# Attention scores as two products of 128 rows: the keys' low part stored twice

## The chip, the core and the metric

The kernel runs on one core of a Trainium2 chip. The core has a matrix engine (TensorE, PE in the profile; its weight loads are a queue of their own, PEld), a vector engine (DVE), a scalar engine (ACT), GpSimd (POOL) and a sync engine (SP) that issues transfers. The metric is the device time of one execution in microseconds (us); for the kernel before, the median of three runs is 3030.7 us (3026.78 to 3032.99).

## What is computed

Two blocks follow each other on 512 latent tokens of width 1024. Block 1 has two layers. Each layer modulates the normed latents and 256 context tokens, projects them, and mixes them by a global attention, a windowed attention with a sink and a short convolution; a mixture of 16 experts follows, in which each expert chooses its tokens. The context has its own mixer and experts in layer 0 alone. Block 2 has a banded attention with a sink, a dilated attention, gates and an output product. The attention at the heart of block 1 is:

```python
def attend(q, k, v, mask, sink):
    s = jnp.einsum('bqkgd,bskd->bkgqs', q, k, preferred_element_type=jnp.float32) * (HEAD_DIM ** -0.5)
    if mask is not None:
        s = jnp.where(mask, s, NEG_INF)
    ...
        p = jax.nn.softmax(s, axis=-1)
    return jnp.einsum('bkgqs,bskd->bqkgd', p.astype(v.dtype), v)
```

Heads have 64 columns (HEAD_DIM = 64). Everything is float32.

## The kernel before

A float32 factor is split into a high and a low part, both in PE's faster float32r format, and a product is made of three: high by high, low by high, high by low (`mm3`, L204 to L206). The scores do this with fewer products. A head has only 64 rows, so one tile of 128 rows holds two parts of the query, stacked: its high part in one half of the partitions and its low part in the other (`q_block`, L465 and L466). The keys' high part is stored twice, in both halves (`k_parts`, L475 and L476), so that one product of 128 rows gives high by high plus low by high (L520). The keys' low part is stored once, in the half in which the query's high part lies (L477), and a second product of 64 rows adds high by low (L521). `row` names that half.

A unit of attention is one head and one tile of 128 queries. `scores` makes its row of scores in PSUM (tile S, two buffers), segment by segment: the latents have two segments a unit (latent keys of 256 to 512 columns, context keys of 256), the context and block 2 have one. A vector operation finds the maximum (L531, or L527 with the mask), ACT takes the exponential (L535 or L537), and DVE or ACT scales the rows (L542 or L544) into P. `turn` transposes P on PE (L140) and ACT copies the result (PT, L563); `pv` multiplies it with the values (L611). `section` runs the units one after the other, with each unit's transposes one unit later, and spreads fillers between them: projections of the next heads, the convolution, the merge of branches. Their weights come by transfers from SP (L191) and are split on ACT (L183) and DVE (L184).

The program text gives the order in which work is offered. A scheduler in the framework may move instructions on an engine by its own costs; each engine runs its list in order. The context's keys and values are made in the latents' pass (`lat_start`), written to DRAM on POOL's queue (L816) and read back for the context's own pass (L671); `key_parts` lists what is written.

Of the kernel before, what the change touches and what calls it, by code (L numbers as in the profile page):

```python
# [18 lines left out]
D = 1024  # L19
KT = 8  # L20
# [9 lines left out]
class Stream:  # L30
    """One of the two token streams: latents or context."""
# [6 lines left out]
class Kernel:  # L38
# [43 lines left out]

    def dense_psum(self, mm=2, s=1024):
        """Banks for products (mm), for scores of s columns (2 tiles) and for transposes (2)."""
        es = ExitStack()
        tc = self.tc
        self.s_cols = s
        self.p_mm = es.enter_context(tc.tile_pool(name="p_mm", bufs=mm, space=PSUM, reuse_waits="tile"))
        self.p_s = es.enter_context(tc.tile_pool(name="p_s", bufs=2, space=PSUM, reuse_waits="tile"))
        self.p_t = es.enter_context(tc.tile_pool(name="p_t", bufs=2, space=PSUM, reuse_waits="tile"))  # L90
        return es
# [14 lines left out]
    def blend(*parts):  # L106
        """The steps of several (generator, steps), spread evenly over each other."""
# [22 lines left out]
    def copy(self, out, in_):  # L130
        """A plain copy, on the scalar engine and the vector engine in turn."""
# [10 lines left out]
    def rsqrt(self, ss, shape, mul, eps):  # L142
        """(ss * mul + eps) ** -0.5 and the radicand, by Newton's iteration."""
# [21 lines left out]
    def exp(self, pool, out, x, w):  # L165
        """exp(x) for x <= 0 on the vector engine, to float32's accuracy: 2^k * e^r, |r| <= ln(2) / 2."""
# [14 lines left out]
    def split(self, src, hi, lo):  # L181
        """src = hi + lo, both in the 12 significant bits of float32r."""
        self.nc.scalar.activation(hi, src, ACTF.Copy)  # L183
        self.nc.vector.tensor_sub(lo, src, hi.bitcast(FP32))  # L184

    def wblock(self, pool, src):
        """A block of weights [K, 256]: per 512 rows its two float32r parts [128, 4, 256]."""
# [10 lines left out]
    def mm3(self, ps, lhs, rhs, lsel, rsel):  # L198
        """ps = sum over k tiles of lhs^T rhs, each a list of two parts by k tile."""
# [70 lines left out]
    def adaln(self, l, r, pool):  # L270
        """Columns r * 2048 to (r + 1) * 2048 of both streams' modulation of layer l, in 17 steps."""
# [35 lines left out]
    def ada_load(self, l, r, pool, *tiles):  # L307
        """Loads pieces [128, 1024] of w_ada, unless they are there."""
# [7 lines left out]

    def affine_cols(self, name, gname, gi, l, s, kinds):
        """The per-channel scale g * (1 + sc) and shift of a modulated norm."""
# [8 lines left out]
    def norm(self, xt, junk, xn=None):  # L327
        """Token-major rows scaled by their rsqrt of the mean square, in place or into xn; the last tile's on its own."""
# [9 lines left out]
    def scale(self, out, in_, col, i):  # L338
        """Rows by a column, on the vector engine and the scalar engine in turn."""
# [17 lines left out]
    def hT(self, pool, h, xn, G, S):  # L357
        """The modulated norm of a stream, channel-major, in two parts; KT steps."""
# [21 lines left out]
    def hT_raw(self, raw, xn):  # L380
        """The norm without its modulation, channel-major."""
# [14 lines left out]

    def rope_tab(self, pool, name, g, tab):
        """Rope's tables with a norm's gain folded in: [128, 4, 64] for x and for its swapped halves."""
# [12 lines left out]
    def heads_block(self, pool, ps, dst, ss, t, nh, tabs, g):  # L411
        """dst = rope(ps * g) for nh heads of one token tile; ss = their sums of squares."""
# [21 lines left out]
    def q_block(self, out, pool, xp, wp, src, h, st, tabs, g, sink, kv=None):  # L434
        """Four query heads, in five steps: two tiles [128, 2, n] of stacked parts, scales and sinks.

        The high parts lie in half kv, or head by head in one and the other.
        """
# [32 lines left out]
    def k_parts(self, tp, kh, kl, j):  # L471
        """Head j of the transposed keys tp [128, n] into the doubled parts kh, kl [128, n]."""
# [4 lines left out]
        nc.vector.tensor_sub(kl[a], tp[a], kh[a].bitcast(FP32))  # L477

    def k_block(self, pool, kr, ss, nt, nh, kh, kl):
        """Normalises the roped keys kr [128, nt, nh * 64] and writes their parts."""  # L480
# [11 lines left out]
    def kv_block(self, pool, w, h, st, tabs, g, kh, kl, V, kr=None):  # L492
        """Two key heads and two value heads of a stream from a block [ka | va] of w_in."""
# [14 lines left out]

    def scores(self, pool, q, row, t, segs, region, mask, sc, skc, mult):
        """Softmax of one head and query tile: its rows [128, keys].  # L510

        row: the rows of the high parts of the queries and the low parts of the keys; segs: (score
        column, key parts, key column, width); region: the score columns in use.
        """
# [4 lines left out]
        for at, kh, kl, k0, w in segs:  # L519
            nc.tensor.matmul(S[:, at:at + w], lhs, kh[:, k0:k0 + w], start=True, stop=False)  # L520
            nc.tensor.matmul(S[:, at:at + w], lhs[row], kl[row, k0:k0 + w], start=False, stop=True)  # L521
# [25 lines left out]
    def turn(self, P, c0, slots, PT, qc):  # L547
        """P's key tiles, transposed, into PT[:, slot, qc:qc + 128]; slots: (score column, slot)."""
# [17 lines left out]
    def section(self, groups, fillers, last=False):  # L566
        """Runs groups of attention units with other work between them.

        groups: an iterable of (units, finish); a unit: (rows, then), where rows() emits the scores
        and the softmax and then(rows) the transposes, which come one unit later; finish comes one  # L570
        step behind the last unit of its group. fillers: (generator, steps).
        """
# [30 lines left out]
    def pv(self, PTs, plans):  # L603
        """O^T [128 = two heads, 256]; a plan: (slot, values, first column, end) by key tile."""
# [11 lines left out]

    def mixer(self, l, st, src, csrc, dst, ahead=None):
        """x + gt1 * mixer(modulated norm of x) for one stream, then the router's choice.

        ahead: how many slots of expert weights to open at the start, behind the attention, behind  # L620
        the merge and behind the projection.
        """
# [110 lines left out]
    def close_above(es, k):  # L733
        """Closes the pools of a stack above its first k."""
# [7 lines left out]
    def lat_start(self, l, wp, xp, kp, h, K, src, csrc):  # L742
        """The latents' modulated norm and keys and values, and the context's; its parts go to DRAM for its own pass."""
# [4 lines left out]
        with ExitStack() as es:  # L748
# [26 lines left out]
            def keys():  # L775
                """Four blocks of keys and values, each one's end behind the next one's products."""
# [48 lines left out]
    def key_parts(K):  # L825
        """The written parts of two branches' keys and values."""
        return [x for kh, kl, V in K for x in (kh, kl[0:64, 0], kl[64:128, 1], V)]
# [9 lines left out]
    def ring_open(self, side, k, first=False):  # L837
        """Opens k slots; with first, the first one lies behind the others."""
# [8 lines left out]
    def ring_fill(self):  # L847
        """Loads into the slots that are open, one a step."""
# [4 lines left out]
    def ring_load(self):  # L853
        """Loads the next half of an expert's matrix into the next slot."""
# [27 lines left out]
    def attention(self, b, kv, ap, qd, K, KC, mask, o, n):  # L882
        """The groups of one attention branch's four heads that share keys: two pairs of heads into o."""
# [7 lines left out]
        def unit(PTs, pr, j, half, ti):  # L891
# [28 lines left out]
            def rows():  # L920
                return self.scores(ap, q[pr][:, j], slice(64 * kv, 64 * kv + 64), t, segs, r, msk,
# [62 lines left out]
    def merge(self, l, st, wp, p, h, W, b, o, acc, step, xp=None, mg=None):  # L984
        """acc += 2 * sigmoid(gate b) * (o @ w_branch[b]); at the last step the halved sum's parts."""
# [30 lines left out]
    def project(self, l, st, wp, p, mg, src, dst, ring, extra):  # L1016
        """x + gt1 * (merged @ w_out), its norm and the router's softmax over the experts [tokens, NE].

        The softmax has the latents' tiles in the order 0, 2, 1, 3.
        """  # L1020
# [20 lines left out]
        def shift():  # L1041
            """The router's share of the norm's shift and its weights with the scale."""
# [6 lines left out]
        def rows(t):  # L1049
            """A tile's logits and normalised rows, in two steps."""  # L1050
# [60 lines left out]
    def choose(self, l, st, p, z):  # L1111
        """Each expert's tokens and gates (halved), by slots: in columns, or as scatter and gather indices.
# [498 lines left out]
```

## Time and profile before

| | |
|---|---|
| median of the runs | 3030.7 us |
| span of the profiled execution | 3023.8 us |
| PE busy | 2895.2 us (96%) |
| PE weight loads busy | 1866.4 us (62%) |
| DVE busy | 1415.6 us (47%) |
| ACT busy | 957.7 us (32%) |

The profile is of one execution, whose own time is given as its span, from the first instruction to the last. The shares are means over stages that differ: attention stands at 135 to 535 us (latents, layer 0), 720 to 880 (context), 1646 to 2046 (latents, layer 1) and 2780 to 2995 (block 2); the experts, with their large weight transfers, lie between. A PE that is shown as busy need not be at its peak, since products overlap and their ends are modelled; what a product costs in a row of products is the distance from its start to the next one's.

### The profile page before, as it was taken

To read this page: it belongs to the slowest core of one execution; us is meant where nothing else is said; L and a number is where in the kernel's file an instruction comes from. 1 tells how busy PE (TensorE), PEld (TensorE's weight loads), DVE (VectorE), ACT (ScalarE), POOL (GpSimd) and SP (SyncE) were. 2 spreads that over 40 slices of the span, in tenths; PEclk is the share of its full clock that TensorE was granted. 3 is DMA by queue.
4 is the path that set the end of the run, shared out by engine and by line. 5 is a ranking of instruction groups with operands and counts; after the bars stand their busy time and mean duration, and the time that the engine had idled before them with its cause. 6 is when DMAs were issued, how large, how long until landed. Compare 5 with 4: busy or idle time off the path is not lost.

```text
span 3023.8 us, 45171 instructions
## 1 busy us (share of the span) xinstructions
PE 2895.2 (96%) x18117; PEld 1866.4 (62%) x18117; DVE 1415.6 (47%) x3807; ACT 957.7 (32%) x1950; POOL 110.1 (4%) x135
## 2 busy tenths in 40 slices
PE   7999999999998999999979999999799999889999
PEld 3777777678895443433347777778744433338878
DVE  4655565348764111111146555654523232237885
ACT  4444454224552000000044444543200000015663
POOL 0100000011001011100000000000000000000000
PEclk8999999999998999999999999999899999999999
DMA  8321111668457999999573211114689999953221
GB/s 296 123 69 56 56 42 50 206 210 308 136 174 255 389 403 397 402 395 368 180 262 116 68 56 56 43 53 141 260 348 397 414 361 363 370 196 107 57 84 57
DMA packets 272646, 629.24 MB, mean 208 GB/s; under 512 B 24324, under 2 KB 148948, under 8 KB 272436
## 3 DMA queue, kind: packets, MB, share of 16 engines
q1 hardware_dynamic: 259396, 595.31, 53.5%
q0 software_dynamic: 12016, 27.86, 3.2%
q8 instruction: 143, 2.34, 0.3%
q10 hardware_dynamic: 1024, 3.18, 0.3%
q14 instruction: 67, 0.55, 0.1%
HBM read 606.30 MB, written 19.99 MB: 207 GB/s over the span
## 4 chain that ended last, share of the span: by engine, by line
PE 73%; issue 14%; DMA 6%; DVE 4%; ACT 1%; SPq 0%; POOL 0%; POOLq 0%; ACTq 0%; DVEq 0%
PE mm L204 13%; PE mm L205 12%; PE mm L206 12%; PE au L1217 8%; PE tp L140 5%; PE yp L1243 4%; PE S L521 4%; PE mm L611 4%; DMA x<-ylat,silat 4%; PE S L520 3%; PE S L282 3%; PE tx L1330 2%; PE yp L1348 1%; DVE xt L1350 1%; PE S L1038 1%
## 5 line engine op out<-in xcount | busy, mean ns | idle before, releaser
L204 PE MATMUL mm<-hhi,whi 128*128 128x512 f32 (+1 forms) x928 | 341.6, 368 | 0.0
L184 DVE TENSOR_TENSOR wlo<-wraw,whi 128x1024 fp32r<-128x1024 f32 x234 | 285.7, 1222 | 107.0 <-ACT whi L183 102.4
L206 PE MATMUL mm<-hhi,wlo 128*128 128x512 f32 (+1 forms) x928 | 335.1, 361 | 0.0
L205 PE MATMUL mm<-hlo,whi 128*128 128x512 f32 (+1 forms) x928 | 333.6, 360 | 0.0
L183 ACT ACTIVATE whi<-wraw 128x1024 fp32r<-128x1024 f32 x234 | 247.1, 1059 | 185.5 <-PE mm L205 106.7
L1243 PE MATMUL yp<-we,hT 128*32 128x256 f32 (+1 forms) x2016 | 294.2, 496 | 10.3 <-ACT hT L134 4.9
L1217 PE MATMUL au<-we,xT 128*64 128x512 f32 x1024 | 236.5, 597 | 0.0
L204 PE MATMUL mm<-whi,hhi 128*128 128x256 f32 x736 | 218.8, 298 | 10.6 <-ACT qr L423 6.6
L1217 PE MATMUL au<-we,xTlat 128*64 128x512 f32 x960 | 227.1, 599 | 0.3
L205 PE MATMUL mm<-wlo,hhi 128*128 128x256 f32 x736 | 212.8, 290 | 2.1 <-DVE wlo L184 2.1
L206 PE MATMUL mm<-whi,hlo 128*128 128x256 f32 x736 | 212.5, 290 | 0.0
L1243 PEld LDWEIGHTS yp<-we,hT 128*32 128x32 f32 (+1 forms) x2016 | 99.1, 124 | 182.4 <-issue 144.5
L563 ACT ACTIVATE PT<-tp 128x384 f32<-128x384 f32 (+2 forms) x392 | 142.6, 407 | 211.6 <-PE tp L140 209.7
L204 PEld LDWEIGHTS mm<-hhi,whi 128*128 128x128 f32 x928 | 176.3, 190 | 32.1 <-issue 4.4
L206 PEld LDWEIGHTS mm<-hhi,wlo 128*128 128x128 f32 x928 | 176.0, 190 | 25.9 <-issue 1.1
L205 PEld LDWEIGHTS mm<-hlo,whi 128*128 128x128 f32 x928 | 176.3, 190 | 24.9 <-issue 1.5
L535 ACT ACTIVATE P<-S,mx,sc 128x768 f32<-128x768 f32 (+5 forms) x192 | 151.9, 792 | 70.9 <-DVE mx L532 67.6
L204 PEld LDWEIGHTS mm<-whi,hhi 128*128 128x128 f32 x736 | 143.0, 194 | 26.9 <-ACT qr L423 8.5
L1217 PEld LDWEIGHTS au<-we,xT 128*64 128x64 f32 x1024 | 70.6, 137 | 129.2 <-issue 126.1
L205 PEld LDWEIGHTS mm<-wlo,hhi 128*128 128x128 f32 x736 | 143.0, 195 | 5.4 <-DVE wlo L184 2.7
L206 PEld LDWEIGHTS mm<-whi,hlo 128*128 128x128 f32 x736 | 142.7, 194 | 4.0 <-issue 2.8
L1226 ACT ACTIVATE th<-au 128x512 f32<-128x512 f32 (+1 forms) x47 | 24.6, 524 | 378.3 <-PE au L1217 378.3
(326 smaller groups left out, 4830.5 us busy)
## 6 DMA issues: line engine op xcount, KB each, us to landing
we<-in_w_e_gate_dram SPq DMA_DIRECT2D x128, 1024.0 KB, 11.5
we<-in_w_e_up_dram SPq DMA_DIRECT2D x128, 1024.0 KB, 11.1
we<-in_w_e_down_dram SPq DMA_DIRECT2D x128, 1024.0 KB, 11.0
wraw<-in_w_in_dram SPq DMA_DIRECT2D x166, 512.0 KB, 3.7
wada<-in_w_ada_dram SPq DMA_DIRECT2D x96, 512.0 KB, 6.1
wraw<-in_w_branch_dram SPq DMA_DIRECT2D x36, 512.0 KB, 3.4
wraw<-in_w_out_dram SPq DMA_DIRECT2D x32, 512.0 KB, 3.9
xt<-in_x_dram SPq DMA_DIRECT2D x8, 512.0 KB, 9.2
```

Of the source, the lines that this page charges most:

```text
L140: self.nc.tensor.transpose(out, in_, self.ident[:p, :p])
L183: self.nc.scalar.activation(hi, src, ACTF.Copy)
L184: self.nc.vector.tensor_sub(lo, src, hi.bitcast(FP32))
L204: nc.tensor.matmul(ps, lh, rh, start=k == 0, stop=False)
L205: nc.tensor.matmul(ps, lh, rl, start=False, stop=False)
L206: nc.tensor.matmul(ps, ll, rh, start=False, stop=k == n)
L521: nc.tensor.matmul(S[:, at:at + w], lhs[row], kl[row, k0:k0 + w], start=False, stop=True)
L535: nc.scalar.activation(P, S[:, c0:c1], ACTF.Exp, bias=mx[:, 1:2], scale=sc, accum_out=mx[:, 2:3])
L563: self.nc.scalar.activation(PT[:, s0:s0 + j - i, qc:qc + 128], tp[:, i * 128:j * 128].rearrange("p (s c) -> p s c", c=128), ACTF.Copy)
L611: nc.tensor.matmul(O[64 * j:64 * j + 64, a:b], v, PTs[j][:, slot, a:b], start=i == 0, stop=i == last, skip_group_check=True)
L1217: self.nc.tensor.matmul(ps[j * st.cap:(j + 1) * st.cap], st.xT[:, kt, s0:s0 + st.cap], w[kt // 4][:, kt % 4, j * st.w:(j + 1) * st.w], sta ...
L1243: self.nc.tensor.matmul(ps[o * st.cap:(o + 1) * st.cap], hT[:, j * 128 + q * st.cap:j * 128 + (q + 1) * st.cap], w[kt // 4][:, kt % 4, o * ...
```

## The change

`k_parts` writes the keys' low part into both halves, with a second subtraction, and the second score product takes all 128 rows of the query tile and of the low part. It then adds high by low and also low by low. `row` goes away, and the third entry of block 2's key lists with it. `key_parts` now names the whole low tile, so that two transfers of one half each become one of both halves, for the store and for the load.

```diff
@@ k_parts
         nc.scalar.activation(kh[b], tp[a], ACTF.Copy)
         nc.vector.tensor_sub(kl[a], tp[a], kh[a].bitcast(FP32))
+        nc.vector.tensor_sub(kl[b], tp[a], kh[b].bitcast(FP32))
@@ scores
-    def scores(self, pool, q, row, t, segs, region, mask, sc, skc, mult):
+    def scores(self, pool, q, t, segs, region, mask, sc, skc, mult):
...
         for at, kh, kl, k0, w in segs:
             nc.tensor.matmul(S[:, at:at + w], lhs, kh[:, k0:k0 + w], start=True, stop=False)
-            nc.tensor.matmul(S[:, at:at + w], lhs[row], kl[row, k0:k0 + w], start=False, stop=True)
+            nc.tensor.matmul(S[:, at:at + w], lhs, kl[:, k0:k0 + w], start=False, stop=True)
@@ key_parts
-        return [x for kh, kl, V in K for x in (kh, kl[0:64, 0], kl[64:128, 1], V)]
+        return [x for kh, kl, V in K for x in (kh, kl, V)]
@@ attention, rows
-                return self.scores(ap, q[pr][:, j], slice(64 * kv, 64 * kv + 64), t, segs, r, msk,
+                return self.scores(ap, q[pr][:, j], t, segs, r, msk,
@@ block2
-                    segs = [(a0, *K[hh][:2], loc[0] * 128, w_)]
+                    segs = [(a0, *K[hh], loc[0] * 128, w_)]
...
-                out.append(list(zip(kh, kl, (0, 1, 0, 1))))
+                out.append(list(zip(kh, kl)))
```

Below line 477 the changed kernel's line numbers are higher by one, and from the score products on by two: L520 becomes L522, L521 L523, L611 L613.

The numbers of products, loads and transposes on PE are the same, and over most of the program their order too. DVE has 26 instructions more, POOL four transfers fewer. In a few places the scheduler sets things in another order. On DVE, in block 2's first section of attention (kx are the keys of the second four heads, tp their transposes, S and mx a unit's scores and maximum), before:

```order
L484 TENSOR_TENSOR qr<-qr,rsq 128x1024
L538 SCALAR_TENSOR_TENSOR P,mx<-P,mulB 128x128
L540 RECIPROCAL mx<-mx 128x1
L477 TENSOR_TENSOR kx<-tp,kx 64x512
L527 ISA S,mx<-S,maskB 128x128
L527 ISA mx 128x1
L532 TENSOR_SCALAR mx<-mx,sc 128x1
L477 TENSOR_TENSOR kx<-tp,kx 64x512 x3
L417 TENSOR_REDUCE qss<-sq 128x4
```

and now:

```order
L477 TENSOR_TENSOR kx<-tp,kx 64x512
L478 TENSOR_TENSOR kx<-tp,kx 64x512
L477 TENSOR_TENSOR kx<-tp,kx 64x512
L478 TENSOR_TENSOR kx<-tp,kx 64x512
L477 TENSOR_TENSOR kx<-tp,kx 64x512
L478 TENSOR_TENSOR kx<-tp,kx 64x512
L477 TENSOR_TENSOR kx<-tp,kx 64x512
L478 TENSOR_TENSOR kx<-tp,kx 64x512
L417 TENSOR_REDUCE qss<-sq 128x4
L529 ISA S,mx<-S,maskB 128x128
L529 ISA mx 128x1
```

The mask of the unit of 128 columns (L527, now L529) stood behind the first head's subtraction and stands now behind all eight.

On PE, in the second section of block 2, around a unit of 384 columns (tp<-ident,P is a transpose of probabilities; L204 to L206 are a projection), before:

```order
L206 MATMUL mm<-whi,hlo 128x256
L520 MATMUL S<-kx,xq 128x384
L140 MATMUL tp<-ident,P 128x128
L521 MATMUL S<-kx,xq 128x384
L204 MATMUL mm<-whi,hhi 128x256
L205 MATMUL mm<-wlo,hhi 128x256
L206 MATMUL mm<-whi,hlo 128x256
```

and now:

```order
L206 MATMUL mm<-whi,hlo 128x256
L522 MATMUL S<-kx,xq 128x384
L523 MATMUL S<-kx,xq 128x384
L204 MATMUL mm<-whi,hhi 128x256
L205 MATMUL mm<-wlo,hhi 128x256
L140 MATMUL tp<-ident,P 128x128
L206 MATMUL mm<-whi,hlo 128x256
```

The transpose went from between the two score products to behind two products of the projection. At the place of the mask above, three transposes that stood behind 20 projection products stand behind 31.

## Rows read from the trace of the kernel before

**Rows 1.** The page: busy us, share of the span, instructions.
```profile
PE 2895.2 (96%) x18117; PEld 1866.4 (62%) x18117; DVE 1415.6 (47%) x3807; ACT 957.7 (32%) x1950; POOL 110.1 (4%) x135
```

**Rows 2.** The page: shares of the chain that ended last, by engine.
```profile
PE 73%; issue 14%; DMA 6%; DVE 4%; ACT 1%; SPq 0%; POOL 0%; POOLq 0%; ACTq 0%; DVEq 0%
```

**Rows 3.** Stretches of attention: length, busy PE, PEld, DVE, ACT, POOL, PEclk, DMA, GB/s.
```profile
135.00:475.00 340.00, 338.58 (x1775) 254.64 (x1774) 201.04 (x461) 157.98 (x316) 0.00 (x0) 0.99 0.18 55
...
720.00:880.00 160.00, 159.95 (x1206) 143.84 (x1205) 123.03 (x360) 89.47 (x184) 0.00 (x0) 1.00 0.56 180
...
2780.00:2995.00 215.00, 212.64 (x1388) 172.60 (x1387) 171.24 (x663) 135.44 (x315) 0.00 (x0) 1.00 0.21 66
```

**Rows 4.** What PE waited for from 135 to 475 us: sum, times, longest.
```profile
PE mm L204 <- ACT qr L423: 1.4, 1, 1.4
```

**Rows 5.** PE in time order, 408 to 411 us: start, us, instruction, shapes.
```profile
408.52 0.27 PE L520 MATMUL S<-xk,xq 128*128 128x256 f32 x1
408.73 0.38 PE L521 MATMUL S<-xk,xq 64*128 64x256 f32 x1
409.04 0.38 PE L520 MATMUL S<-kc,xq 128*128 128x256 f32 x1
...
409.66 0.51 PE L204 MATMUL mm<-o,whi 128*128 128x512 f32 x1
410.00 0.40 PE L205 MATMUL mm<-o,whi 128*128 128x512 f32 x1
410.24 0.40 PE L206 MATMUL mm<-o,wlo 128*128 128x512 f32 x1
```

**Rows 6.** Weight loads (PEld) in the same stretch.
```profile
408.29 0.19 PEld L520 LDWEIGHTS S<-xk,xq 128*128 128x128 f32 x1
408.73 0.18 PEld L521 LDWEIGHTS S<-xk,xq 64*128 64x128 f32 x1 [0.25 <-issue]
```

**Rows 7.** PE in time order, block 2, a projection of 256 columns.
```profile
2758.35 0.28 PE L206 MATMUL mm<-whi,hlo 128*128 128x256 f32 x1
2758.47 0.28 PE L204 MATMUL mm<-whi,hhi 128*128 128x256 f32 x1
```

**Rows 8.** PE in time order, second expert stage, products of 64 rows.
```profile
2233.59 0.40 PE L1348 MATMUL yp<-ylo,two 64*128 64x512 f32 x2
2233.82 0.39 PE L1348 MATMUL yp<-yhi,two 64*128 64x512 f32 x1
```

**Rows 9.** PE in time order, a unit of 512 and 256 columns.
```profile
183.37 0.39 PE L520 MATMUL S<-xk,xq 128*128 128x512 f32 x1
...
184.12 0.39 PE L520 MATMUL S<-kc,xq 128*128 128x256 f32 x1
184.75 0.88 PE L140 MATMUL tp<-ident,P 128*128 128x128 f32 x6
```

**Rows 10.** The 64-row score products: ns min/median/max, first and last start, forms.
```profile
L521 PE MATMUL S<-xk,xq x160: 379/440/617, 136.1 to 2036.9; 64*128 64x512 f32 x64, 64*128 64x256 f32 x64, 64*128 64x384 f32 x32
...
L521 PE MATMUL S<-kc,xq x128: 378/381/580, 136.8 to 2036.3; 64*128 64x256 f32 x128
...
L521 PE MATMUL S<-kx,xq x64: 323/382/501, 2781.5 to 2992.7; 64*128 64x256 f32 x32, 64*128 64x128 f32 x16, 64*128 64x384 f32 x8, 64*128 64x512 f32 x8
```

**Rows 11.** The subtraction that makes a low part, by shape.
```profile
L477 DVE TENSOR_TENSOR kx<-tp,kx x10: 675/688/694, 2759.9 to 2882.7; 64x512 fp32r<-64x512 f32 x10
```

**Rows 12.** DVE in time order, block 2, second key block.
```profile
2815.93 0.68 DVE L477 TENSOR_TENSOR kx<-tp,kx 64x512 fp32r<-64x512 f32 x1 [1.74 <-ACT kx L476]
2816.53 0.28 DVE L527 CUSTOM_DVE_ANT_0 S<-S,maskB 128x128 f32<-128x128 f32 x1
...
2818.37 0.69 DVE L477 TENSOR_TENSOR kx<-tp,kx 64x512 fp32r<-64x512 f32 x1 [0.54 <-ACT kx L476]
```

**Rows 13.** Block 2: probabilities done on DVE, and their transpose on PE.
```profile
2962.45 0.29 DVE L542 TENSOR_SCALAR P<-P,mx 128x129 f32<-128x129 f32 x1
...
2962.96 0.33 PE L140 MATMUL tp<-ident,P 128*128 128x128 f32 x1
```

More of the change, by code (lines that the diff above doesn't have):

```diff
@@ L1440, in rows @@
                     def rows():
-                        return self.scores(ap, q[pr][:, j], slice(64 * K[hh][2], 64 * K[hh][2] + 64), t, segs, r, msk,
+                        return self.scores(ap, q[pr][:, j], t, segs, r, msk,
                                            sc[:, t, hh:hh + 1], sk_, mul)
@@ L1548, in block2 @@
                 Vh = [V_[:, t, kv * 64:kv * 64 + 64] for t in range(4)]
-                self.section(attend(Qs.pop(0), [(kh[:, kv], kl[:, kv], kv)] * 4, [Vh] * 4, 0, 2 * kv, Gs[2 + kv]),
+                self.section(attend(Qs.pop(0), [(kh[:, kv], kl[:, kv])] * 4, [Vh] * 4, 0, 2 * kv, Gs[2 + kv]),
                              fill[kv], last=kv == 1)
```

## The prediction

> **What bounds the kernel now.** I read the page first: TensorE (PE) is busy 2895 of the 3024 us, the vector engine (DVE) 1416 [rows 1]. A busy PE can still be a waiting one, so I read the chain that ended last: 73% of it is PE and another 14% "issue", time in which an engine waited for nothing that the profile shows [rows 2]. Then I cut out the stretches in which scores are made. In the latents' attention of layer 0 (135 to 475 us, with a tail to 535) PE is busy 339 of 340 us, DVE 201, the scalar engine (ACT) 158, at a granted clock of 0.99, so nearly all of it at 2.4 GHz. In the context's attention (720 to 880) PE is full and DVE busy 77%, in block 2 (2780 to 2995) PE 99% and DVE 80% [rows 3]. Last I asked what PE waits for in the first stretch: one wait of 1.4 us [rows 4]. So in all these places PE's own rate sets the time, and what the change takes from PE there is taken from the end, until something else gets late.
>
> Now the score products themselves [rows 5]. What counts is the distance from one start to the next. In a unit of 256-wide scores the starts are 408.52, 408.73 and 409.04, and 409.66 for the next other product: 0.21, 0.31, and 0.62 us for the two after. Products of 128 rows and 256 columns that follow each other start 0.12 apart [rows 7], and of 512 columns 0.23 to 0.24 (410.00 to 410.24). Each step into or out of the 64-row product is thus 0.09 to 0.19 dearer than its columns. The weight loads tell why [rows 6]: the 128-row load starts at 408.29, 0.23 ahead of its product, and is hidden behind the product before, but the 64-row load starts at 408.73, with its own product, after 0.25 us of idle. The 64 rows as such are not slow: where 64-row products follow 64-row products, in the second expert stage, two of 512 columns stand as one group at 2233.59 and the next starts 0.23 later, at 2233.82 [rows 8]. The price is the switch between the two shapes, and the change removes every switch at the scores.
>
> **The change part by part.**
>
> *Second product of 64 rows becomes one of 128.* Per unit in the latents with 256 + 256 columns: from 408.52 to 410.00 (the start of the second wide product, which is also late, 0.34 instead of 0.23) it takes 1.48; without switches 4 x 0.12 + 0.24 = 0.72. That frees 0.76. A unit with 512 + 256 columns, followed by transposes, takes 183.37 to 184.75 = 1.38 [rows 9]: 0.75 for the first pair and 0.63 for the second, against 0.52 and 0.62 above; without switches 2 x 0.23 + 2 x 0.12 = 0.70, so 0.68. There are 352 pairs (160 + 128 + 64, the first at 136.1, the last at 2992.7) [rows 10]: 256 in the latents' two layers, two pairs a unit, so 128 units; 32 in the context and 64 in block 2, one pair a unit. By these rows: latents 128 x 0.72 = 92 us; a single pair of 256 columns gives 0.21 + 0.31 - 0.24 = 0.28, or 0.38 with the late follower, say 0.33: context 32 x 0.33 = 11, block 2 64 x 0.33 = 21. Sum 124. Reading the starts of all 704 score products in this way, instead of these samples, gives 122 at the products and 15 at their followers, 137 in all (latents 100, context 12, block 2 25). I take 137, since it holds every width, and keep 124 as the lower reading.
>
> *One more subtraction per key head on DVE.* 26 of them, 0.688 for one of 64x512 [rows 11] and no more for the eight of half the width: at most 17.9 us of DVE work. What hides it is PE's own work in the key stages and DVE's idle 41% in the latents [rows 3]; without that cover it costs all 17.9. Bounds 0 and 17.9; I take 3, nearer to 0, because PE's waits show nothing of the present subtraction in the latents' stretch [rows 4], and because DVE idles about 0.5 us ahead of each for the scalar engine's second copy (0.54 before 2818.37) [rows 12]. What is queued behind it on DVE: the rope of the query heads, and in block 2 a mask. The order of DVE shows it: the mask of 128x128 stood behind one of four key heads and now stands behind all four with their doubles, eight subtractions and not one. In the trace it ran at 2816.53 [rows 12]; four heads of 2 x 0.688 from 2815.93 on end at 2821.4. So this unit's probabilities can come up to 5 us late. The order of PE moves the same way: transposes of probabilities stand some products further back, at that place 11 products of 0.12, 1.3 us. Two of block 2's three key blocks have masks behind them (the first is done before any score); I count 2 us for each, 4 in all.
>
> *What gets late next.* With PE faster, the softmax has less time. In block 2 it is already close: probabilities are done at 2962.45 + 0.29 = 2962.74, and their transpose starts at 2962.96, 0.22 later [rows 13]. Read so for each unit, from the first at 2788.4 to the last at 2996.2, half of block 2's 64 units have under 0.5 us there, and each loses 0.33 to 0.38 of PE work: I give back 7 of the 25. In the context, where a sixth of the units are that tight, 2 of 12; in the latents, where nine units in ten have over 0.8, 4 of 100.
>
> *DMA, POOL.* The low key parts of the context go to DRAM and back in one transfer and not in two halves: four issues fewer on POOL's queue, twice the bytes for that tile. POOL's stores wait for DVE's second subtraction, under 0.69 later, with only stores queued behind them; they are read back in the context's own pass, a whole mixer later. I cost it at nothing. The weights' stream is not the limit in the attention stretches (DMA share 0.18 to 0.56) [rows 3].
>
> Sum: 137 - 3 - 4 - 7 - 2 - 4 = 117 off the profiled span of 3023.8. That execution's span lies 6.9 us under the median of 3030.7, which also holds what is outside the span; I subtract from the median: **2914 us**. Own range: 2893 (all 137 carried) to 2942 (124, with all 17.9 of the subtractions exposed and the other 17 of losses).
>
> **The rivals.**
>
> *The softmax takes over.* If DVE's queue sets the pace once PE is 14% faster, waits for probabilities or for copies of transposes replace the switches. For it: block 2's 80% on DVE, which becomes some 90% of a shorter stretch; against it: 59% in the latents, with room behind almost every unit. If half of the 137 goes this way: 3030.7 - 68 = 2962, own range 2935 to 2990.
>
> *Loads that hide only across row groups.* The second product might be bound by its own weight load, which shares all rows with the product before: 0.19 load [rows 6] + 0.11 for 256 columns (half of 0.23 for 512) = 0.30 for each, about the 0.31 of today. Then 704 x 0.01 = 7 us come off, and the subtractions give 3 to 18 back: about 3030. Against it: 128-row products with new weights each do start 0.12 apart [rows 7], and their loads do start early [rows 6]. The Trainium skill has this as a rule ("TensorE: Matmul & The Clock Gate", Part 3, The mechanism): a weight load overlaps products in flight only when the row group differs. Here the trace disagrees with it, as the 0.12 shows.
>
> *Slower.* The time at the score products is no switch but belongs to two products into the same columns of PSUM with the same query tile, and stays; then only the 26 subtractions are new, in the key stages and ahead of block 2's masks, where the first score of each section waits for both low halves: 3030.7 + 17.9 = 3049. It decides only if the switches give under 18 us. Against it: other products into one PSUM tile (L204 to L206) go at 0.12 [rows 7].
>
> *More than the reading.* Transposes that now stand between or right behind the pair get cheaper too, and a shorter stretch: 2880 to 2893.
>
> **How the numbers follow.** Forecast 0.74, more than the reading 0.06, softmax 0.12, loads 0.04, slower 0.04. The range that leaves out no more than 2 in 10 goes from 2893 to 2950: the forecast's own and the upper half of its unknown costs, with the near part of the softmax case. About 0.2% (6 us) is what a measurement of this kernel can tell from no change. Faster by more than that: 0.74 + 0.06 + 0.12 and a little of the loads' case, 0.93; within it 0.03; slower 0.04.
>
> **What would show it.** Right: score products start 0.12 (256 columns) and 0.23 (512) apart, their loads start with the product before, the product behind them is not late, and the latents' attention is about 48 us shorter in each layer, the context's 10, block 2's 14. The softmax rival: the starts are so, but transposes of probabilities show waits on DVE or ACT of 0.3 us a unit in the latents. The loads' rival: starts 0.30 apart, loads starting with their own product. Wrong altogether: stretches outside attention that change by more than some us, or a lower granted clock in them.

## The result

The changed kernel takes 2923.36 us (median of 4 runs, 2918.15 to 2923.75) against 3031.84 for the kernel before in the same set of runs; the ratio is 0.9644 with a 95% interval of 0.9629 to 0.9659. The forecast was 2914, so the direction and the mechanism held, and the sum was 9 us too good. A second set of five runs on another occasion gave 2917.43 (2915.89 to 2918.52), ratio 0.9635 (0.9616 to 0.9654).

The page of the changed kernel (busy us, share of the span, instructions), to lay beside [rows 1]:

```profile
span 2916.4 us, 45194 instructions
...
PE 2777.7 (95%) x18117; PEld 1842.6 (63%) x18117; DVE 1422.9 (49%) x3833; ACT 955.9 (33%) x1950; POOL 107.7 (4%) x131
```

The span fell by 107.4 us and busy PE by 117.5, with the same 18117 products; DVE has its 26 instructions more and is busy 7 us longer. The mean granted clock is 0.977 in both profiled executions; where it was low differs between them, though, and that has a small part in what follows.

Next, PE in time order in the unit that [rows 5] show, now at 381.72 (start, us, instruction, shapes):

```profile
381.72 0.28 PE L522 MATMUL S<-xk,xq 128*128 128x256 f32 x1
381.83 0.28 PE L523 MATMUL S<-xk,xq 128*128 128x256 f32 x1
381.95 0.28 PE L522 MATMUL S<-kc,xq 128*128 128x256 f32 x1
382.07 0.28 PE L523 MATMUL S<-kc,xq 128*128 128x256 f32 x1
382.19 0.40 PE L204 MATMUL mm<-o,whi 128*128 128x512 f32 x1
382.42 0.39 PE L205 MATMUL mm<-o,whi 128*128 128x512 f32 x1
```

and its weight loads:

```profile
381.72 0.19 PEld L523 LDWEIGHTS S<-xk,xq 128*128 128x128 f32 x1
381.83 0.19 PEld L522 LDWEIGHTS S<-kc,xq 128*128 128x128 f32 x1
381.95 0.19 PEld L523 LDWEIGHTS S<-kc,xq 128*128 128x128 f32 x1
382.07 0.19 PEld L204 LDWEIGHTS mm<-o,whi 128*128 128x128 f32 x1
```

The starts are 0.11 to 0.12 apart, the wide product behind the unit is no longer late (382.19 to 382.42, 0.23), and each load starts with the product before its own: the load of 381.95 belongs to the product of 382.07. From the first score to the start of the second wide product the unit took 1.48 and takes 0.70; the forecast's working had 0.72.

How far that reaches is read from the distance between the first and the last score product of each stretch:

| us | first score at | latents, layer 0 | context | latents, layer 1 | block 2 |
|---|---|---|---|---|---|
| before | 135.6 | 391.5 | 157.1 | 390.2 | 211.4 |
| after | 138.3 | 346.5 | 149.1 | 346.5 | 198.8 |
| change | +2.7 | -45.0 | -8.0 | -43.7 | -12.6 |
| forecast | | -48 | -10 | -48 | -14 |

All four stretches together lose 109.3 us. Part of that is the clock. In the kernel before, PE was granted half its clock (1.2 GHz in place of 2.4) for some 7 us of layer 0's latents, although it had been busy for 235.9 of the 237.3 us ahead of them. Experiment 1 below, whose products there are the same in the same order, had the full clock throughout. The rows give length, busy PE, PEld, DVE, ACT and POOL, PEclk, DMA and GB/s, for the kernel before and then for experiment 1:

```profile
372.90:379.80 6.90, 6.90 (x27) 4.72 (x29) 4.42 (x19) 0.98 (x2) 0.00 (x0) 0.51 0.00 0
```

```profile
139.24:527.60 388.36, 386.95 (x2032) 289.12 (x2032) 230.48 (x538) 185.01 (x378) 0.00 (x0) 1.00 0.17 55
```

The two runs drift apart by 3.1 us, and all of it within those 7. So 41.9 of the 45.0 us in layer 0 are the change's. In layer 1 the kernel before has a piece of low clock half as long, and the changed kernel has none in either layer. For that piece 1.5 us is an estimate, from experiment 5, where layer 0's latents with one piece of that length took 389.9 in place of 388.4. At equal clock the four stretches thus lose some 105 us.

In the changed kernel the distances repeat well: in its second trace they are 346.5, 149.9, 346.6 and 198.8. The stages between them, with their large weight transfers, do not: the one from the context to layer 1 took 779.3 and 776.2, and 771.8 to 779.5 in the variants below, at a granted clock of 0.97 in the first trace and 0.98 in the one with 771.8. Whole times go with the clock too: the first set has 2918.15 at a mean of 0.977 and 2923.27 to 2923.75 at 0.975, the second, 6 us lower in the median, 0.977 to 0.978 throughout. A few us are therefore read from the stretches and not from whole times.

### The profile page after: what moved, and what is told of

Same layout as the page of the kernel before. It is cut to its first block, busy times and chain, and to the rows that moved or that the text cites. A ratio compares the mean times of both kernels' runs of the same rounds, so it can differ in the third digit from the quotient of the medians.

```text
span 2916.4 us, 45194 instructions
## 1 busy us (share of the span) xinstructions
PE 2777.7 (95%) x18117; PEld 1842.6 (63%) x18117; DVE 1422.9 (49%) x3833; ACT 955.9 (33%) x1950; POOL 107.7 (4%) x131
## 5 line engine op out<-in xcount | busy, mean ns | idle before, releaser
L204 PE MATMUL mm<-hhi,whi 128*128 128x512 f32 (+1 forms) x928 | 340.2, 367 | 0.0
L206 PE MATMUL mm<-hhi,wlo 128*128 128x512 f32 (+1 forms) x928 | 335.1, 361 | 0.0
L204 PE MATMUL mm<-whi,hhi 128*128 128x256 f32 x736 | 216.2, 295 | 10.0 <-ACT qr L423 5.1
L205 PE MATMUL mm<-wlo,hhi 128*128 128x256 f32 x736 | 211.5, 289 | 1.6 <-DVE wlo L184 1.6
L206 PE MATMUL mm<-whi,hlo 128*128 128x256 f32 x736 | 211.8, 289 | 0.0
L204 PEld LDWEIGHTS mm<-hhi,whi 128*128 128x128 f32 x928 | 176.8, 191 | 29.5 <-issue 4.9
L206 PEld LDWEIGHTS mm<-hhi,wlo 128*128 128x128 f32 x928 | 176.4, 190 | 26.0 <-issue 0.8
L204 PEld LDWEIGHTS mm<-whi,hhi 128*128 128x128 f32 x736 | 142.3, 193 | 22.8 <-ACT qr L423 7.4
L1219 PEld LDWEIGHTS au<-we,xTlat 128*64 128x64 f32 x960 | 64.7, 136 | 127.3 <-issue 120.0
```

The lines of the kernel that those rows point to most:

```text
L204: nc.tensor.matmul(ps, lh, rh, start=k == 0, stop=False)
L205: nc.tensor.matmul(ps, lh, rl, start=False, stop=False)
L206: nc.tensor.matmul(ps, ll, rh, start=False, stop=k == n)
L1219: self.nc.tensor.matmul(ps[j * st.cap:(j + 1) * st.cap], st.xT[:, kt, s0:s0 + st.cap], w[kt // 4][:, kt % 4, j * st.w:(j + 1) * st.w], sta ...
```

## Experiments

Each was timed beside the kernel before (medians of 3027 to 3030 us in the three sets). "Lag" is the number of units by which transposes stand behind their scores.

**1. The subtractions alone** (the kernel before with the 26 subtractions; the second product stays at 64 rows).

```diff
         nc.vector.tensor_sub(kl[a], tp[a], kh[a].bitcast(FP32))
+        nc.vector.tensor_sub(kl[b], tp[a], kh[b].bitcast(FP32))
```

> The kernel before with the 26 added subtractions alone (the low part is stored twice, the second product still reads 64 rows of it). Theory, the subtractions lie beside PE's work: 3 us slower than before, 0 to 6, the first score of layer 0 at about 138 instead of 135.6 us, score products as before. Rival, the subtractions stand on the path: 18 us slower, 3049.

Measured: 3032.07 us, ratio 1.0015 (1.0003 to 1.0027), 1 to 8 us slower. The stretches stay (388.4, 156.9, 390.0, 212.1; the first differs from 391.5 by the clock, as said above), and the first score comes at 139.2 in place of 135.6. What PE waits for in that key stage, from 60 to 140 us, in this kernel (waited for, sum, times, longest):

```profile
PE mm L204 <- ACT qr L423: 1.8, 2, 1.5
PE tp L140 <- DVE qr L432: 1.2, 1, 1.2
PE mm L204 <- ACT whi L183: 1.1, 1, 1.1
PE mm L204 <- ACT Vctx L503: 0.7, 1, 0.7
PE tp L140 <- DVE krlat L485: 0.3, 1, 0.3
```

and in the kernel before:

```profile
PE mm L204 <- ACT qr L423: 1.7, 2, 1.5
PE mm L205 <- DVE wlo L184: 0.5, 1, 0.5
PE mm L204 <- ACT whi L183: 0.4, 1, 0.4
```

5.1 us of waits against 2.6. So the subtractions are hidden in the attention stretches and cost a few us in the key stages, where PE now waits for the rope (L432) and the scaling of the keys (L485) on DVE as well. That the subtractions ahead of them hold them up is read from DVE's order and was not tried by itself. Waiting is not all of the cost: the clock has a part in it as well (next section). The 17.9 us of the slower rival is out.

**2. Fewer switches, same products** (the kernel before with both 128-row products of a latent unit first, then both 64-row ones; 64-row products, subtractions and all else as before).

```diff
         for at, kh, kl, k0, w in segs:
             nc.tensor.matmul(S[:, at:at + w], lhs, kh[:, k0:k0 + w], start=True, stop=False)
+        for at, kh, kl, k0, w in segs:
             nc.tensor.matmul(S[:, at:at + w], lhs[row], kl[row, k0:k0 + w], start=False, stop=True)
```

> The kernel before with the four score products of a latent unit in another order: both of 128 rows, then both of 64, so two switches of shape a unit instead of four, with the same products. Theory, the switch is the price: a later pair's 0.31 + 0.31 becomes 0.12 + 0.12, so 0.38 a unit, 128 units, 49 us less a few for waits: about 2985 (2975 to 2995); context and block 2 unchanged. Rival, 64-row products are dear in themselves: no change, 3032. Rival, two products in a row into the same columns are dear: all of the latents' 92 us, about 2940.

Measured: 2977.68 us, ratio 0.9833 (0.9816 to 0.985), 50 us faster, with the latents at 363.7 and 367.0 and the context and block 2, which have one pair a unit, unchanged (157.1, 211.5). PE in this kernel, the unit that answers to [rows 5]:

```profile
389.14 0.28 PE L520 MATMUL S<-xk,xq 128*128 128x256 f32 x1
389.26 0.28 PE L520 MATMUL S<-kc,xq 128*128 128x256 f32 x1
389.46 0.38 PE L522 MATMUL S<-xk,xq 64*128 64x256 f32 x1
389.69 0.28 PE L522 MATMUL S<-kc,xq 64*128 64x256 f32 x1
389.89 0.50 PE L204 MATMUL mm<-o,whi 128*128 128x512 f32 x1
390.23 0.39 PE L205 MATMUL mm<-o,whi 128*128 128x512 f32 x1
```

and its loads:

```profile
388.91 0.19 PEld L520 LDWEIGHTS S<-xk,xq 128*128 128x128 f32 x1
389.14 0.19 PEld L520 LDWEIGHTS S<-kc,xq 128*128 128x128 f32 x1
389.46 0.18 PEld L522 LDWEIGHTS S<-xk,xq 64*128 64x128 f32 x1
389.57 0.19 PEld L522 LDWEIGHTS S<-kc,xq 64*128 64x128 f32 x1
```

Inside a pair of one shape the second load starts ahead of its product (389.14 for 389.26, 389.57 for 389.69); at the step into the 64 rows it starts with it (389.46). The unit takes 1.09 where it took 1.48, with the same four products into the same PSUM columns. The price is on the switch: half the switches gone gave 51.0 us in the latents, where the change, with none left, gave 88.7. Neither the 64 rows nor the shared columns of PSUM carry it.

**3. No second subtraction** (the changed kernel with the unused half of the low tile filled with zeros by GpSimd; low by low, which the kernel before does not compute either, is left out).

```diff
-        nc.vector.tensor_sub(kl[b], tp[a], kh[b].bitcast(FP32))
+        nc.gpsimd.memset(kl[b].bitcast(FP32), 0.0)
```

> The changed kernel with zeros in the second half of the low part, written by GpSimd, in place of the second subtraction (high by low alone, as before the change). Theory, the subtractions cost 3 at the key stages and some more ahead of block 2's masks: 2923.4 - 5 = 2918 (2915 to 2921). Rival, they are hidden altogether: 2923. Rival, GpSimd is late with its zeros and scores wait: slower than 2924.

Measured: 2915.43 us, ratio 0.9621 (0.96 to 0.9643). The first score is back at 135.3, the latents are at 346.5 and the context at 149.6; the stage into layer 1 is 1.7 us shorter, which is less than it varies by. The whole time is 8 us under the first set of the changed kernel and 2 under the second, so it says little by itself. Block 2 gains only 0.8 (198.0), and this is the place where the masks were feared for. DVE in the changed kernel, the place of [rows 12]:

```profile
2719.32 0.68 DVE L477 TENSOR_TENSOR kx<-tp,kx 64x512 fp32r<-64x512 f32 x1 [1.63 <-ACT kx L476]
...
2725.62 0.30 DVE L529 CUSTOM_DVE_ANT_0 S<-S,maskB 128x128 f32<-128x128 f32 x1
```

and in experiment 3:

```profile
2718.09 0.68 DVE L477 TENSOR_TENSOR kx<-tp,kx 64x512 fp32r<-64x512 f32 x1 [1.63 <-ACT kx L476]
2718.69 0.28 DVE L529 CUSTOM_DVE_ANT_0 S<-S,maskB 128x128 f32<-128x128 f32 x1
```

The mask does come 6.3 us behind the first subtraction in the changed kernel, against 0.6, as read from the order. But PE has its projection to do in that time, and its longest wait there, 0.84 us for the subtractions, is there in both kernels ("PE tp L140 <- DVE kx" 0.8 in each). A mask that is 5 us late was nearly free.

**4. Two units of lag in the context and block 2** (the changed kernel; P gets a third buffer in those stages, which the output tile og gives up).

```diff
-        self.pend = None
+        self.pend, self.lag = [], 1
...
-        P = pool.tile([128, self.pcols], FP32, name="P", bufs=2)[:, :c1 - c0]
+        P = pool.tile([128, self.pcols], FP32, name="P", bufs=1 + self.lag)[:, :c1 - c0]
...
-                prev, self.pend = self.pend, (then, r, finish if k == len(units) - 1 else None)
+                self.pend.append((then, r, finish if k == len(units) - 1 else None))
+                prev = self.pend.pop(0) if len(self.pend) > self.lag else None
```

> The changed kernel with the transposes of probabilities two units behind their scores instead of one, in the context and block 2 alone (three buffers of probabilities, one of block 2's gated outputs). Theory, what the change did not bring there (context 8 of 12 us, block 2 13 of 25) went into transposes that wait for probabilities: 8 to 14 us come back, 2910 to 2916. Rival, it went elsewhere (copies of transposes, or the reading of the starts was too high): within 3 us of 2923.

Measured: 2911.41 us, ratio 0.9614 (0.9597 to 0.9631); the context 3.0 us shorter (146.1) and block 2 5.4 (193.4). The wait that the lag takes away looks like this in the changed kernel, block 2, PE and then DVE:

```profile
2869.45 0.28 PE L205 MATMUL mm<-wlo,mxh 128*128 128x256 f32 x1
2869.99 0.41 PE L140 MATMUL tp<-ident,P 128*128 128x128 f32 x2 [0.26 <-DVE P L544]
```

```profile
2869.49 0.36 DVE L544 TENSOR_SCALAR P<-P,mx 128x257 f32<-128x257 f32 x1
```

P is done at 2869.85 and the transpose starts at 2869.99: 0.14 behind it and 0.54 behind the product before, of which 0.12 was that product's own. The waits of PE in block 2 (2686 to 2888) show only a part, because the modelled end of the product before covers the beginning of a wait:

```profile
PE mm L613 <- ACT PT L565: 1.3, 3, 0.5
PE tp L140 <- DVE P L544: 1.1, 3, 0.7
PE tp L140 <- ACT P L546: 1.0, 3, 0.5
PE tp L140 <- DVE kx L478: 0.8, 1, 0.8
```

In the kernel of experiment 4 (2682 to 2880) the two lines on P are gone:

```profile
PE tp L140 <- ACT PT L565: 1.2, 2, 0.9
PE tp L140 <- DVE qr L485: 0.8, 2, 0.5
PE S L522 <- ACT P L539: 0.8, 1, 0.8
PE tp L140 <- DVE kx L478: 0.5, 1, 0.5
```

**5. The control: the same lag in the kernel before** (the edit of experiment 4, with the 64-row products).

> The kernel before, with its 64-row products, and with the transposes of the context and block 2 two units behind. Theory (the waits for probabilities are new with the change, since the switches of row shape gave the softmax time): little to gain, 0 to 4 us of 3030, and the stretches of the context and block 2 stay within 2 us each of 157 and 211. Rival (a longer lag helps these stretches whatever the score products are): as much as in the changed kernel, 8 us in the two stretches together, 3019 to 3022.

Measured: 3020.68 us, ratio 0.9976 (0.9962 to 0.999). Context 154.2 and block 2 207.7: 2.9 and 3.7 us shorter. The theory missed here: 6.6 of the 8.4 us that the lag gave the changed kernel were to be had without the change. Part of that is a wait that has nothing to do with scores: value products that waited 1.2 us in block 2 for copies of transposes in the kernel before (L611 for PT) do so no more. So the gain of experiment 4 is not proof that the change's loss lay there; that is read from the waits themselves, below.

**6. The latents' transposes behind the step's fillers** (the changed kernel; some 20 to 25 products later, and the finish of a pair of heads one step later).

```diff
-                if prev is not None:
+                if prev is not None and not self.behind:
                     prev[0](prev[1])
...
+                if self.behind:
+                    if self.fin is not None:
+                        self.fin()
+                    self.fin = None
+                    if prev is not None:
+                        prev[0](prev[1])
+                        self.fin = prev[2]
```

> The changed kernel (2923.4), in which the transposes of a unit's probabilities in the two latents' stretches come behind the step's fillers, about 20 to 25 products later on TensorE, and the finish of a pair of heads one step later; the context and block 2 are as in the changed kernel. Theory (the 5 us per layer that the latents' stretches still lack, 45 and 44 instead of 48 to 50 us shorter, are transposes that come up to probabilities not yet done, since under the changed kernel 32% of them stand within 0.5 us of their probabilities): both latents' stretches get 3 to 5 us shorter, 346.5 to some 342, and the time is 2913 to 2918. Rival (the missing part is elsewhere, in the neighbours' own pace): the stretches stay within 1 us of 346.5 and the time within 3 us of 2923.

Measured: 2911.08 us, ratio 0.9623 (0.9604 to 0.9641), with the latents 1.6 and 2.4 us shorter (344.9 and 344.1). Median and stretches did not agree, so this kernel, the changed kernel and a third were timed again side by side.

> The latents' transposes behind the step's fillers, again. Its trace shows the two latents' stretches 1.6 and 2.4 us shorter and the context's 0.8, while its median is 12 us under that of the changed kernel's first runs. Theory (what is in the stretches is all of it): 4 to 6 us under the changed kernel of this call. Rival (some 12 us, of which part lies outside the attention stretches): 10 to 13 us under it.

> The changed kernel itself, beside the two variants below on one chip, since the variants so far were compared with it across two calls, whose runs of the kernel before differ by 3 us in the median. 2918 to 2924 by its four runs of 2923.4; its four stretches as in its first trace (346.5, 149.1, 346.5, 198.8 us).

Measured: 2916.86 us (2909.49 to 2917.14) against 2917.43 for the changed kernel. The 12 us between the first medians were the difference of two sets of runs. Neither the theory's 4 to 6 us under the changed kernel nor the rival's 10 to 13 was met; the profiled execution, at 2909.49, is the odd one of the five. The stretches repeat (344.9 and 345.0): the edit moves 1.5 to 2.4 us a layer (1.5 or 1.6 where a piece of low clock falls into the stretch, 2.4 where none does), and the rest of the missing 4 to 5 lies elsewhere. In its first trace no transpose behind a projection waits for P any more, but the query's low parts still hold some up (0.7 us in layer 0, 1.4 in layer 1; the next section tells how that is read). The new neighbours cost nothing on balance: transposes now follow value products, a step between shapes as well (last section), and in each layer 14 of them start 2.5 us late in sum, but the 14 score products that stood there in the changed kernel were late by 2.6.

**7. The edits together.** Zeros and the lag of two:

> The changed kernel with both earlier edits: the unused half of the low key tile is filled with zeros by GpSimd in place of the second subtraction, and in the context and block 2 the transposes come two units behind their scores. Alone the first gave 8 us (2915.4) and the second 12 (2911.4). Theory (the two act in different places: the zeros in the key stages, the lag in the context and block 2): the gains add, 2923.4 - 8 - 12 = 2903, between 2900 and 2907, with key stages of 135 and 777 us before the first scores and stretches of 146 and 193 us in the context and block 2. Rival (part of both gains is the same wait, probabilities held up behind the doubled subtractions in block 2): about 2910, and block 2 stays at 193.

Measured: 2909.04 us, ratio 0.9609 (0.959 to 0.9627); first score at 135.2, context 146.7, block 2 193.2. The first key stage and the stretches are as the theory had them, to within 1 us, though block 2 keeps nothing of the zeros' 0.8. The whole time is nearer to the rival's 2910: the theory's 2903 had been put together from medians of different sets, whose gains of 8 and 12 us were larger than the stretches had shown (5 and 8).

All three:

> The changed kernel with all three edits: zeros by GpSimd, the context and block 2 two units behind, and the latents' transposes behind the step's fillers. Theory (all three losses are separate): 2903 less the 6 to 10 us of the latents, 2893 to 2898, which would be the whole 137 us of the row shapes from the kernel before. Rival (the latents' transposes wait for nothing that matters): as without the third edit, about 2903.

> Zeros by GpSimd, the context and block 2 two units behind, the latents' transposes behind the fillers, again. Its trace against that of the changed kernel: key stages 4.2 and 1.3 us shorter, stretches 1.6, 1.1, 2.4 and 5.6 us shorter, 16 in all. Theory (the sum of the stretches): 13 to 18 us under the changed kernel of this call. Rival (20 us, as the medians of two calls differ): 19 to 22 under it.

Measured: 2903.16 us and, in the second set, 2905.24 (2900.91 to 2907.09), ratios 0.9595 (0.9577 to 0.9613) and 0.9591 (0.9571 to 0.961). That is 12.2 us under the changed kernel timed on the same chip, with no overlap between the two, and the fastest kernel of this study. The rival's 2903 of the first expectation was met in number only. It gave the third edit nothing, but beside 2909.04 for the first two edits in the same set the third is worth 5.9 us, 4.0 of it in the latents (344.9 and 344.1); the theory had the 6 to 10 about right and started from too low a time. The 13 to 18 of the second expectation was a little high.

## Why the prediction was right, and where its sum was off

For each product of the four stretches I took the distance to the next start and subtracted what a row of like products shows (0.12 us for 256 columns, 0.23 for 512). What is left, in us, sorted by what follows what:

| beyond a regular row | latents 0 | context | latents 1 | block 2 | change, all |
|---|---|---|---|---|---|
| behind a score product: before, after | 46.0, 3.1 | 10.1, 1.2 | 45.4, 3.1 | 20.0, 5.0 | -109.1 |
| transposes of P behind a projection or merge product | 0.7, 3.4 | 0.4, 2.3 | 0.8, 3.4 | 2.0, 6.5 | +11.7 |
| all else | 9.9, 5.1 | 5.8, 4.8 | 8.9, 5.1 | 11.3, 9.2 | -11.7 |

*The price is a switch of shape, and it goes.* Shown, by the starts in the changed kernel and by experiment 2, which gets over half of the gain in the latents by halving the switches. [rows 8] bear it out, though not quite as they were read: the two products of that group use different halves of the rows and start 0.01 us apart, so that they run side by side; the single products behind them stand 0.22 to 0.24 apart. **The gross term was too large**: of the 122 us at the score products 109 came off and 12.4 stay, the largest part in block 2 (5.0); of the 15 at their followers at most 11.7 came off, since the last row of the table holds other gaps too, 2.3 us of the clock in layer 0 among them. So at most 121 and not 137, some 116 at equal clock, below even the sample reading of 124. The mistake was to count every gap down to the regular distance, as if nothing stood behind the switch.

That the sum missed by only 9 us is in part luck. The gross term was 16 us too high, and the losses, 20 us, were too high as well: late transposes took 11.7, the first key stage 2.7, and the stages between the stretches, which vary, gave 0.9 back.

*Subtractions, 3.* They cost 2.7 us in the first key stage: the first score stands at 134.1 to 136.5 us in the seven traces without them and at 137.3 to 139.7 in the six with them. The second key stage lies in a stage that varies by more than they cost, and alone they cost 4.5 us (1 to 8) in experiment 1. So the size was about right, as far as these runs can tell; the cover of PE's own work in the key stages, which the prediction counted on, is the one that failed, while DVE's idle time in the latents held. The prediction did not have the clock in it: from 60 to 135 us the granted clock is 0.98 in each of the six traces and 1.00 in each of the seven. The changed kernel, and the kernel before:

```profile
60.00:135.00 75.00, 71.21 (x445) 53.78 (x445) 49.80 (x170) 30.43 (x69) 14.10 (x26) 0.98 0.52 177
```

```profile
60.00:135.00 75.00, 72.28 (x457) 54.36 (x456) 46.51 (x163) 32.61 (x73) 15.19 (x28) 1.00 0.55 186
```

In the first trace of the changed kernel the products from 116.94 to 120.34, of 256 columns, start 0.21 apart and not 0.12, which makes 1.5 us. In its second trace the clock is low earlier (0.83 from 80 to 90 us), and PE waits 1.2 us for the rope as well, as in experiment 1. What brings the clock down was not tried.

*Masks, 4.* Too much. The late mask is there, but experiment 3 gives back 0.8 us in all of block 2. The order was read rightly and its price was not: 11 products of delay cost next to nothing when the products before them are work that must be done anyway.

*What gets late next, 13 (7, 2 and 4).* Transposes that start late because of others grew by 11.7 us in sum. Block 2 got 4.5 and not 7, the context 1.9 for 2, the latents 5.3 and not 4. The tails of these gaps tell whom they wait for: a transpose starts 0.15 us after the end of a DVE instruction or 0.05 after one of ACT. By that mark 5.6 us of block 2's late transposes wait for P (1.1 before; those behind score products are counted here too), 1.7 of the context's, and 1.5 in each of the latents' layers. In the latents nearly half is due to something that the prediction did not name: the query's low parts. PE, then DVE, in the changed kernel:

```profile
383.56 0.40 PE L204 MATMUL mm<-o,whi 128*128 128x512 f32 x1
384.30 0.52 PE L140 MATMUL tp<-ident,P 128*128 128x128 f32 x3 [0.34 <-DVE xq L466]
```

```profile
381.40 0.49 DVE L544 TENSOR_SCALAR P<-P,mx 128x513 f32<-128x513 f32 x1
...
382.53 0.67 DVE L466 TENSOR_TENSOR xq<-tp,xq 64x512 fp32r<-64x512 f32 x1
...
383.46 1.30 DVE L466 TENSOR_TENSOR xq<-tp,xq 64x512 fp32r<-64x512 f32 x2
```

P is done at 381.89, 2.4 us ahead; the transposes wait until the first of the two subtractions at 383.46 has read its transpose tile tp in PSUM. The same place in the kernel before has its transposes at 411.40, 0.23 behind the product before, with no wait. Five such places a layer make 1.7 us. Waits for P make no more than 1.5 us a layer, so experiment 6, which was aimed at them, could not get back the missing 5.

*The rivals.* Softmax taking over: its mark, waits of 0.3 us a unit in the latents, is not there; the late transposes are 14 in the 64 units of layer 0's stretch and sum to 3.7 us. Loads hidden only across row groups: out, by loads that start 0.11 to 0.23 ahead of their products although all of them use all rows, and by experiment 2, where the 64-row pair does the same; the rule of the Trainium skill ("TensorE: Matmul & The Clock Gate", Part 3, The mechanism), that a load overlaps products in flight only where the row group differs, does not describe this kernel. Slower: the subtractions cost 4.5 and not 17.9 (experiment 1), and the same columns of PSUM cost nothing (experiment 2).

*What stays open.* The 2.4 us a layer that stay between the score products lie in 25 of 193 distances, 0.08 to 0.11 each; 22 of these come right behind value products or transposes, and none behind another score product. They look like steps of the same kind, but no run took them away. Nor was it tried what brings the clock down, which moved layer 0's latents by 3 us; the stage into layer 1, which differs by up to 7.7 us between traces, was not taken apart.

## What to carry to other kernels

Read a product's price from the distance to the next start, with its neighbours: here a product of half the rows between full ones cost more than a full one, and filling it up (or putting products of one shape together, which gave over half of it in the latents) was a gain, because PE was the bound. Count only part of such a sum: here an eighth of the gaps stayed, almost as much again turned into waits for buffers and probabilities, and the extra vector work cost most in the stage that makes the operand, not in the one that uses it. Before a few us are put down to a change, look at the granted clock of the same stretch in both traces. An operation that stands later in an engine's order is late only if someone waits for it; look at what the waiting engine has to do meanwhile, and try a remedy on the kernel before as well, since most of the lag's gain was there already.

## What the runs showed of the hardware

The step between shapes is not one of rows alone. The value products fill 64 of the 128 columns of the array (128\*64), and the steps into and out of them have the same mark. PE and then its loads, in the changed kernel, behind a group of value products that ends at 372.1:

```profile
372.31 0.39 PE L522 MATMUL S<-kc,xq 128*128 128x256 f32 x1
372.53 0.28 PE L523 MATMUL S<-kc,xq 128*128 128x256 f32 x1
372.65 0.28 PE L522 MATMUL S<-xk,xq 128*128 128x256 f32 x1
```

```profile
372.31 0.19 PEld L522 LDWEIGHTS S<-kc,xq 128*128 128x128 f32 x1 [0.17 <-issue]
372.42 0.19 PEld L523 LDWEIGHTS S<-kc,xq 128*128 128x128 f32 x1
```

The load starts with its product after 0.17 us of idle, and the second score product comes 0.22 behind the first, where the next stands 0.12 behind it. That it is the same thing is read from this mark; no run here tried to remove these steps.

The other finding is how exactly a wait can be read: a transpose held up by DVE starts 0.14 to 0.15 us after the end of the instruction it waits for (2869.85 to 2869.99 above), whether or not the view of waits names it. Where an idle time is shorter than the modelled end of the product before, this mark finds what the view of waits does not show: for P in block 2 it gives the 5.6 us above, where that view has 2.1 (the two lines shown with experiment 4).
